# A two-layer encoder trunk on one core: the MLP's first product token-major, its convolution through DRAM copies, the gated result transposed

## The chip, the cores and the metric

The kernel runs on one core of a Trainium2 chip. The metric is the device time of one execution in microseconds (us): 2912.17 as the median of three runs, 2911.9 to 2914.39.

Names used throughout: PE is TensorE (matmuls), PEld its weight loads, DVE is VectorE, ACT is ScalarE, POOL is GpSimd, SP is SyncE. SP and POOL do no arithmetic here; they issue DMAs, each in the order of its own queue. SBUF is the on-chip memory of 128 partitions, PSUM the memory into which PE accumulates, DRAM the memory outside.

## The reference, cut to what matters

Two layers, each of three sub-layers (token mixing, cross-attention to a memory, a gated MLP), on 256 tokens of 2048 channels in float32. The change concerns the MLP:

```python
def conv_ffn(h, w_up, conv_w, conv_b, w_down):
    u = h @ w_up
    up = jnp.pad(u, ((0, 0), (1, 1), (0, 0)))
    u = up[:, :-2] * conv_w[0] + up[:, 1:-1] * conv_w[1] + up[:, 2:] * conv_w[2] + conv_b
    gate, val = u[..., :D_FF], u[..., D_FF:]
    return (jax.nn.gelu(gate, approximate=True) * val) @ w_down
```

`w_up` is 2048 x 11264 and `w_down` 5632 x 2048 (`D_FF` is 5632). So the first product has 11264 columns, 5632 for the gate and 5632 for the value. The convolution runs over tokens, three taps per channel, and the MLP is wrapped in two RMS norms:

```python
        h = rms_norm(x, ffn_pre_g[l])
        y = conv_ffn(h, w_up[l], conv_w[l], conv_b[l], w_down[l])
        x = x + rms_norm(y, ffn_post_g[l])
```

## The kernel before

**Precision.** Float32 matrices are multiplied as sums of two reduced-precision parts, hi and lo: `x` is rounded to hi, and lo is the rest. A product takes three terms: hi times hi, hi times lo, lo times hi. Weights arrive from DRAM in tiles of 128 x 1024 (512 KB, `load`, L110, issued by SP); ACT makes hi (a cast, L133) and DVE makes lo (a subtraction, L134). There are four buffers each for the loaded tile, hi and lo. Two tiles are a unit of 2048 columns. Activations stand as operands with channels on the partitions: `A_ff` is 16 row tiles of 128 channels, each hi and lo of 256 tokens.

**Two forms of product.** In the *feature-major* form (`block`, L148, called by `ws_chunk`, L163) the weights are loaded into PE and the tokens stream: L151 multiplies hi of the weights by hi and lo of the tokens in one matmul of 512 columns, L152 lo of the weights by hi of the tokens, 256 columns. The result has channels on the partitions. `merge` (L220) then adds the two halves. In the *token-major* form (`mm_rows`, L296) the tokens are loaded into PE, 128 at a time, and 512 weight columns stream: three matmuls, L301 to L303, for each of the two groups of 128 tokens. The result has tokens on the partitions. `projected` (L611) makes one column of 512 output channels in this form out of four units; `stream` (L639) runs a list of such units, makes the next unit (load, cast, split) before it uses the present one, and calls a function `between` after each row tile, into which other work is put.

**The MLP before.** The first 512 columns of `w_up`, the gate and value parts of the first two tiles of 128 channels, are token-major and belong to the sub-layer boundary (`Columns`, `boundary`), where the residual is renewed and the new operand is built; they are turned by eight transposes (L1233, `ut`). All others, 84 chunks of 128 channels per layer, are feature-major (`up`, tile `up`). With channels on the partitions, the convolution runs along the free dimension: `conv` multiplies by the norm's factor (L1190, `rb`), does the middle tap and the bias on ACT (L1192) and the outer taps on DVE as two shifted multiply-adds (L1195, L1199) with one number per channel. GELU (L1223), product (L1224) and `split` (L228, L229) give tiles of `G`, which are already in operand form for the down projection. After each quarter of `G` (11 row tiles) `products` (L371) runs that part of the down projection token-major (tile `y`), in four columns of 512 channels, and adds it up (L1252, L1254, `Out.take`).

**What sets the order.** The program is written as one sequence; a scheduler of the framework moves instructions within limits, engine by engine, before the run. On the chip each engine then works strictly in its order, and waits where an operand is not there. Only in `boundary` is the order that of the text. A layer's end prepares the first weights of the next product ahead (`ahead_apart`), and `products` holds the last matmuls of its last column back so that one group of tokens ends early.

## Time and profile before

The profiled execution took 2912.27 us, of which the profile's span covers 2910.5.

| | before |
|---|---|
| median of three runs | 2912.17 us |
| profiled execution | 2912.27 us |
| its span | 2910.5 us |
| granted TensorE clock, mean | 0.999 |
| DMA traffic, mean | 193 GB/s |
| chunks of the first product, feature-major, per layer | 84 |
| token-major columns of the first product, per layer | 1 |

A row of a group reads: line, engine, operation, tile written <- tiles read, shape out<-in, xcount | time the engine was busy with them, mean ns of one | idle time of the engine just before them and what ended it. A row of the timeline reads: start (us from the span's start), duration, engine, line, operation, count. A row on DMA issues ends with the KB of one and the median us from its issue to its landing. A stretch gives busy us of each engine. PE's matmuls are pipelined, so their durations overlap and sums of them exceed the time; the distance between starts tells the rate.

### The profile page before, as it was taken

What the parts mean: (1) busy time and instruction counts of PE and PEld (TensorE: products, weight loads), DVE (VectorE), ACT (ScalarE), POOL (GpSimd) and SP (SyncE); (2) the same over time, 40 slices, a digit from 0 to 9 for tenths busy, and PEclk for the clock granted to TensorE, in tenths of its full rate; (3) what the DMA queues carried; (4) which work ended last, traced back from release to release, by engine and by line L of the source; (5) the groups of instructions that cost most, each with busy time, mean ns of one, the idle gap of its engine ahead of it and who ended that gap; (6) DMA issues with size and microseconds to landing.
All of it is one profiled execution on the core that took longest, in us unless ns stands there. A gap on an engine that the chain in (4) does not pass through costs nothing.

```text
span 2910.5 us, 39133 instructions
## 1 busy us (share of the span) xinstructions
PE 2897.6 (100%) x14476; PEld 2443.7 (84%) x14476; DVE 2053.4 (71%) x2930; ACT 1583.6 (54%) x2479; POOL 34.9 (1%) x60
## 2 busy tenths in 40 slices
PE   9999999999999999999999999999999999999998
PEld 7888888888888888888878888888888888888887
DVE  6668767666875867767776587776678768677676
ACT  6556455555655545545555564445566555455454
POOL 0000000000000000000000000000000000000000
PEclk9999999999999999999999999999999999999999
DMA  8644776765666566565655456677556666666655
GB/s 290 188 148 159 232 235 224 226 187 160 196 184 195 187 188 191 180 200 184 212 174 182 145 163 222 222 236 215 181 159 202 187 193 186 188 190 186 195 185 163
DMA packets 161775, 563.09 MB, mean 193 GB/s; under 512 B 18480, under 2 KB 19504, under 8 KB 161584
## 3 DMA queue, kind: packets, MB, share of 16 engines
q1 hardware_dynamic: 156816, 545.53, 59.5%
q0 software_dynamic: 4480, 14.68, 1.8%
q8 instruction: 113, 1.85, 0.3%
q14 instruction: 78, 0.64, 0.1%
q10 hardware_dynamic: 288, 0.39, 0.0%
HBM read 556.34 MB, written 4.19 MB: 193 GB/s over the span
## 4 chain that ended last, share of the span: by engine, by line
PE 97%; DVE 1%; ACT 1%; DMA 0%; issue 0%; DVEq 0%; ACTq 0%
PE up L151 22%; PE up L152 11%; PE y L302 8%; PE y L303 8%; PE y L301 8%; PE g L301 4%; PE g L303 4%; PE g L302 4%; PE qk L302 3%; PE qk L303 3%; PE qk L301 2%; PE a L301 2%; PE a L303 2%; PE a L302 2%; PE as L302 2%; PE as L301 2%
## 5 line engine op out<-in xcount | busy, mean ns | idle before, releaser
L134 DVE TENSOR_TENSOR wlo<-w,whi 128x1024 fp32r<-128x1024 f32 (+1 forms) x981 | 1179.9, 1205 | 656.4 <-ACT whi L133 649.4
L133 ACT CAST whi<-w 128x1024 fp32r<-128x1024 f32 (+1 forms) x981 | 1015.6, 1037 | 955.6 <-PE y L303 295.4
L151 PE MATMUL up<-A_ff,whi 128*128 128x512 f32 x2688 | 946.3, 397 | 0.0
L152 PE MATMUL up<-A_ff,wlo 128*128 128x256 f32 x2688 | 755.0, 281 | 0.0
L151 PEld LDWEIGHTS up<-A_ff,whi 128*128 128x128 f32 x2688 | 504.9, 188 | 121.9
L152 PEld LDWEIGHTS up<-A_ff,wlo 128*128 128x128 f32 x2688 | 509.0, 189 | 0.4
L301 PE MATMUL y<-whi,G 128*128 128x512 f32 x704 | 274.3, 390 | 0.0
L302 PE MATMUL y<-wlo,G 128*128 128x512 f32 x704 | 274.2, 389 | 0.0
L303 PE MATMUL y<-whi,G 128*128 128x512 f32 x704 | 274.2, 389 | 0.0
L301 PE MATMUL g<-whi,A_mix 128*128 128x512 f32 x512 | 202.3, 395 | 0.0
L302 PE MATMUL g<-wlo,A_mix 128*128 128x512 f32 x512 | 200.8, 392 | 0.0
L303 PE MATMUL g<-whi,A_mix 128*128 128x512 f32 x512 | 200.3, 391 | 0.0
L303 PEld LDWEIGHTS y<-whi,G 128*128 128x128 f32 x704 | 132.2, 188 | 27.5
L301 PEld LDWEIGHTS y<-whi,G 128*128 128x128 f32 x704 | 132.2, 188 | 27.4
L302 PEld LDWEIGHTS y<-wlo,G 128*128 128x128 f32 x704 | 132.2, 188 | 27.2
L303 PE MATMUL qk<-whi,A_mix 128*128 128x512 f32 x320 | 125.6, 392 | 0.0
L302 PE MATMUL qk<-wlo,A_mix 128*128 128x512 f32 x320 | 125.4, 392 | 0.0
L301 PE MATMUL qk<-whi,A_mix 128*128 128x512 f32 x320 | 124.9, 390 | 0.0
L223 ACT COPY t<-up 128x256 f32<-128x256 f32 x168 | 61.7, 367 | 102.8 <-DVE G L229 84.7
L303 PEld LDWEIGHTS g<-whi,A_mix 128*128 128x128 f32 x512 | 96.3, 188 | 19.1
L301 PEld LDWEIGHTS g<-whi,A_mix 128*128 128x128 f32 x512 | 96.3, 188 | 18.4
L302 PEld LDWEIGHTS g<-wlo,A_mix 128*128 128x128 f32 x512 | 96.4, 188 | 17.9
(264 smaller groups left out, 4076.7 us busy)
## 6 DMA issues: line engine op xcount, KB each, us to landing
w<-in_w_up SPq DMA_DIRECT2D x336, 512.0 KB, 4.5
w<-in_w_dn SPq DMA_DIRECT2D x160, 512.0 KB, 4.0
w<-in_w_g SPq DMA_DIRECT2D x128, 512.0 KB, 4.3
w<-in_w_qk SPq DMA_DIRECT2D x80, 512.0 KB, 4.5
w<-in_w_ao SPq DMA_DIRECT2D x64, 512.0 KB, 5.0
w<-in_w_mo SPq DMA_DIRECT2D x64, 512.0 KB, 4.3
w<-in_w_vu SPq DMA_DIRECT2D x47, 512.0 KB, 4.5
w<-in_w_fo SPq DMA_DIRECT2D x32, 512.0 KB, 4.1
```

Source lines behind the costliest of these rows:

```text
L133: nc.scalar.copy(hi[:, :m], w[:, :m])
L134: nc.vector.tensor_sub(lo[:, :m], w[:, :m], hi[:, :m].bitcast(F32))
L151: nc.tensor.matmul(ps, hi, a, start=first, stop=False, skip_group_check=True)
L152: nc.tensor.matmul(ps[:, :T], lo, a[:, 0:T], start=False, stop=last, skip_group_check=True)
L223: nc.scalar.copy(b, ps[:, T : 2 * T])
L301: nc.tensor.matmul(ps, ah, hi, start=first, stop=False)
L302: nc.tensor.matmul(ps, ah, lo, start=False, stop=False)
L303: nc.tensor.matmul(ps, al, hi, start=False, stop=last)
```

## The change

All but the first 512 columns of `w_up` become token-major as well, as 21 further halves per layer of 512 columns (11 blocks of 512 channels, each a gate half and a value half; the gate half of block 0 is the boundary's). Each half is a `projected` item list of four units. After a half, ACT evicts both groups of tokens with the norm's factor (now a number per partition) into one of four places, `gate`, `val`, `left`, `right`. As tokens are now on the partitions, the convolution's neighbours lie on other partitions: POOL stores the half (256 x 512, 512 KB) into a DRAM tile `bounce` with a row of zeros at either end, and reads it back twice, shifted by one row, into `left` and `right`. The taps and the bias, now rows of 512 numbers, are loaded by SP to all partitions (`taps`, 1 MB per half). DVE multiplies the three copies by their taps and adds them; GELU is on ACT, the product with the gate on DVE. `turn` transposes the value half on PE, four transposes for each group of tokens, into a PSUM tile `gt`, from which ACT and DVE make hi and lo of `G`. A list `due` spreads these steps over the row tiles of the next half: each is called so many row tiles after the half's end (the middle tap at 5, left 9, right 10, sums 11 and 12, GELU or product 13, turns 14 and 15). The down projection runs after the gate halves of blocks 4 and 8 (16 row tiles each, of blocks 0 to 3 and 4 to 7, as further items of the same stream) and at the end (12 row tiles, by `products`, which takes the first eight row tiles of columns 0 and 1 first and calls `beside` after each row tile). `par` loses the taps; the host lays weights out anew.

The core of the diff:

```diff
-    def products(src, S, nk, begin, finish, last, ahead=(), made=None, mid=None):
+    def products(src, S, nk, begin, finish, last, ahead=(), made=None, mid=None, first=None, beside=None):
         late = []
-        for n in range(4):
-            begin(n)
-            pss = [psum(f"y{j}") for j in range(2)]
+        order = [(n, k0) for n in range(4) for k0 in range(0, nk, 4)]
+        if first is not None:
+            order.sort(key=lambda u: (u[0] > 1, u[0] < 2 and u[1] >= first, u))
...
+                if beside is not None:
+                    beside()
...
+    bounce = [dram.tile([T + 2, 512], F32, tag=f"bounce{i}", name="bounce", bufs=1) for i in range(2)]
+    zeros = cp.tile([2, 512], F32, tag="zeros", name="zeros")
+    nc.vector.memset(zeros, 0.0)
+    for rows in bounce:
+        nc.gpsimd.dma_start(rows[0:1], zeros[0:1])
+        nc.gpsimd.dma_start(rows[T + 1 : T + 2], zeros[1:2])
...
+        def beside(i=None):
+            now = [f for n, f in due if n == 1]
+            due[:] = [(n - 1, f) for n, f in due if n > 1]
+            for f in now:
+                f()
+
+        def taps(i):
+            if not places:
+                c, d = [big.tile([P, 8, 512], F32, tag=tag, name=name) for tag, name in (("C", "cv"), ("D", "uv"))]
+                places.update(taps=(c[:, 0:4], c[:, 4:8]), gate=d[:, 0:2], val=d[:, 2:4], left=d[:, 4:6], right=d[:, 6:8])
+            b, w = divmod(i, 2)
+            h = b + w * NB
+            to = places["taps"][w]
+            nc.sync.dma_start(to, t["conv"][l, :, h * 512 : (h + 1) * 512].partition_broadcast(P))
+            return to
+
+        def half(i):
+            b, w = divmod(i, 2)
+            def finish(j, ps, to):
+                u = places["val" if w else "gate"]
+                nc.scalar.activation(u[:, j], ps, AF.Copy, scale=pre.t[:, j : j + 1])
+                if not j:
+                    return
+                left, right = places["left"], places["right"]
+                rows = bounce[w]
+                nc.gpsimd.dma_start(rows[1 : T + 1].rearrange("(j p) n -> p j n", j=2), u)
+                nc.gpsimd.dma_start(left, rows[0:T].rearrange("(j p) n -> p j n", j=2))
+                nc.gpsimd.dma_start(right, rows[2 : T + 2].rearrange("(j p) n -> p j n", j=2))
+                def times(v, k):
+                    nc.vector.tensor_mul(v, v, to[:, k : k + 1].to_broadcast([P, 2, 512]))
+                def own():
+                    times(u, 1)
+                    nc.vector.tensor_add(u, u, to[:, 3:4].to_broadcast([P, 2, 512]))
+                def activate():
+                    if w:
+                        nc.vector.tensor_mul(u, u, places["gate"])
+                    else:
+                        nc.scalar.activation(u, u, AF.Gelu_apprx_tanh)
+                due.extend([(5, own), (9, lambda: times(left, 0)), (10, lambda: times(right, 2))])
+                due.extend([(n, lambda v=v: nc.vector.tensor_add(u, u, v)) for n, v in ((11, left), (12, right))])
+                due.append((13, activate))
+                if w:
+                    due.extend([(14, lambda: turn(0)), (15, lambda: turn(1))])
+
+            def turn(j):
+                q, k = divmod(b, DN)
+                if G[q] is None:
+                    G[q] = big.tile([P, 4 * min(DN, NB - q * DN), 2, T], F32R, tag="B", name="G")
+                pt = ps_sc.tile([P, 4, P], F32, tag="sc", name="gt")
+                for m in range(4):
+                    nc.tensor.transpose(pt[:, m], places["val"][:, j, m * P : (m + 1) * P], ident)
+                hi, lo = [G[q][:, 4 * k : 4 * k + 4, part, j * P : (j + 1) * P] for part in range(2)]
+                nc.scalar.copy(hi, pt)
+                nc.vector.tensor_sub(lo, pt, hi.bitcast(F32))
+            return finish
+
+        def up(i):
+            b, w = divmod(i, 2)
+            return projected(t["w_up"][l, b + w * NB], A, "up", half(i), lambda: taps(i))
...
+        for i in range(1, 2 * NB):
+            items += up(i)
+            b = i // 2
+            if i % 2 == 0 and b % DN == 0:
+                q = b // DN - 1
+                for n in range(4):
+                    src = down(q, n)
+                    items += projected([src[:, u * UW : (u + 1) * UW] for u in range(4)], Down(q), "y", sum_down(q, n))
...
+        steps = products(
+            [down(2, n) for n in range(4)], Down(2), 4 * (NB - 2 * DN), y.gain, lambda j, n, ps: y.take(j, n, ps, True), 4,
+            before_last, items[-1].w, mid=5, first=8, beside=beside,
+        )
```

Three places in the new order follow. In the names, `up0` and `up1` are the PSUM tiles of the two groups of tokens, `whi`, `wlo` and `w32` a weight tile's hi, lo and loaded form, `con` holds the identity, `cv` the taps, and `uv` all four places; a word such as DVE_49 or DMASW7_49 in brackets is the semaphore of an engine or DMA queue waited for.

TensorE, in layer 0's first product. Before, the end of one chunk of 128 channels (`up_8590`) and the start of the next (`up_8645`):

```order
L151 MATMUL up_8590<-A_ff_5930,whi_8586 128x512
L152 MATMUL up_8590<-A_ff_5930,wlo_8587 128x256
L151 MATMUL up_8590<-A_ff_5930,whi_8586 128x512
L152 MATMUL up_8590<-A_ff_5930,wlo_8587 128x256
L151 MATMUL up_8645<-A_ff_5930,whi_8637 128x512 [waits Activation_49]
L152 MATMUL up_8645<-A_ff_5930,wlo_8638 128x256 [waits DVE_49]
```

Now, near the end of the gate half of block 2 (`up0_6886`, `up1_6887`): the end of its seventh weight tile, 6954, and the first half of its eighth, 6958:

```order
L302 MATMUL up1_6887<-whi_6954,A_ff_5938 128x512
L303 MATMUL up1_6887<-wlo_6955,A_ff_5938 128x512
L304 MATMUL up1_6887<-whi_6954,A_ff_5938 128x512
L1275 MATMUL gt_7016<-con_95,uv_6322 128x128 [waits DVE_49,PE_49]
L1275 MATMUL gt_7016<-con_95,uv_6322 128x128 x3
L302 MATMUL up0_6886<-whi_6958,A_ff_5938 128x512 [waits Activation_49]
L303 MATMUL up0_6886<-wlo_6959,A_ff_5938 128x512
L304 MATMUL up0_6886<-whi_6958,A_ff_5938 128x512
L302 MATMUL up1_6887<-whi_6958,A_ff_5938 128x512
```

The feature-major matmuls are gone; the first turn of block 1's value half stands after seven of the eight weight tiles and waits for DVE, with the eighth tile's matmuls behind it.

VectorE, the same half: from the split of its fifth weight tile (6917) to the product with the gate. The tiles 6921, 6955 and 6959 are its sixth to eighth, 6996 is the first of the next half.

```order
L135 TENSOR_TENSOR wlo_6917<-w32_6912,whi_6916 128x1024 [waits DMAHW3_49,Activation_49]
L1251 TENSOR_TENSOR uv_6322<-uv_6322,cv_6321 128x1024 [waits DMAHW1_49,DMASW7_49]
L1255 TENSOR_TENSOR uv_6322<-uv_6322,cv_6321 128x1024 [waits DVE_49]
L135 TENSOR_TENSOR wlo_6921<-w32_6914,whi_6920 128x1024 [waits DMAHW4_49,Activation_49]
L1251 TENSOR_TENSOR uv_6322<-uv_6322,cv_6321 128x1024 [waits DMASW0_49]
L135 TENSOR_TENSOR wlo_6955<-w32_6950,whi_6954 128x1024 [waits DMAHW5_49,Activation_49]
L1251 TENSOR_TENSOR uv_6322<-uv_6322,cv_6321 128x1024 [waits DMASW1_49]
L1264 TENSOR_TENSOR uv_6322<-uv_6322 128x1024 [waits DVE_49]
L135 TENSOR_TENSOR wlo_6959<-w32_6952,whi_6958 128x1024 [waits DMAHW6_49,Activation_49]
L1264 TENSOR_TENSOR uv_6322<-uv_6322 128x1024 [waits DVE_49]
L135 TENSOR_TENSOR wlo_6996<-w32_6991,whi_6995 128x1024 [waits DMAHW7_49,Activation_49]
L1259 TENSOR_TENSOR uv_6322<-uv_6322 128x1024 [waits DVE_49]
```

The three rows of L1251 are the middle tap (it waits for the store, as it overwrites what is stored), the left and the right copy (they wait for their reads). Between the left copy and the product stand three splits of weights, and the product is what the turn above waits for.

GpSimd, two halves in a row (`bounce_325` takes value halves, `bounce_324` gate halves); before, its queue held nothing in this stretch.

```order
L1246 DMA bounce_325<-uv_6322 128x2x512 [waits DMASW2_49,DMASW3_49,DVE_49,Activation_49]
L1247 DMA uv_6322<-bounce_325 128x2x512 [waits DMASW7_49,DVE_49]
L1248 DMA uv_6322<-bounce_325 128x2x512 [waits DVE_49]
L1246 DMA bounce_324<-uv_6322 128x2x512 [waits DMASW6_49,DMASW5_49,Activation_49]
L1247 DMA uv_6322<-bounce_324 128x2x512 [waits DMASW2_49,DVE_49]
L1248 DMA uv_6322<-bounce_324 128x2x512 [waits DVE_49]
```

The store waits for the eviction on ACT, the first read for the store's landing (DMASW7 in the second row), and the second read follows the first in the queue.

More of the change, by code (lines that the diff above doesn't have):

```diff
@@ L1276, in encoder @@
+        steps = products(
+            [down(2, n) for n in range(4)], Down(2), 4 * (NB - 2 * DN), y.gain, lambda j, n, ps: y.take(j, n, ps, True), 4,
+            before_last, items[-1].w, mid=5, first=8, beside=beside,
+        )
+        for n in range(4):
+            next(steps)
         if l + 1 < L:
@@ L1397, in _layout @@
         st["w_xo"].append(_rows(i["w_xo"][l]))
[L1398 to L1402 removed]
+        st["w_up"].append(_outer(i["w_up"][l]))
+        st["w_dn"].append(_rows(i["w_down"][l]))
     a["par"] = par
```

201 lines of the change are left out of this document (81 added, 120 removed).

## The prediction

> **What bounds the kernel now.** I read the page first (busy shares and the chain that ended last), then stretches, then single instructions in the timeline.
>
> ```profile
> PE 2897.6 (100%) x14476; PEld 2443.7 (84%) x14476; DVE 2053.4 (71%) x2930; ACT 1583.6 (54%) x2479; POOL 34.9 (1%) x60
> PE 97%; DVE 1%; ACT 1%; DMA 0%; issue 0%; DVEq 0%; ACTq 0%
> 750.00:860.00 110.00, 110.00 (x624) 96.55 (x623) 91.41 (x149) 67.46 (x108) 0.00 (x0) 1.00 0.60 186
> ```
>
> The chain is TensorE almost alone. The third row is a stretch inside the MLP (us, then busy time of PE, PEld, DVE, ACT, POOL, then clock, DMA share, GB/s): PE never waits, VectorE works 91 of 110 us, the DMA engines 60%. So the first question is how fast matmuls follow each other, the second whether the new work can make PE wait.
>
> Durations of matmuls overlap, so I count starts. The first two rows are 27 pairs of the feature-major product apart, the last two 18 token-major matmuls:
>
> ```profile
> 999.87 0.40 PE L151 MATMUL up<-A_ff,whi 128*128 128x512 f32 x1
> ...
> 1009.41 0.40 PE L151 MATMUL up<-A_ff,whi 128*128 128x512 f32 x1
> ...
> 299.73 0.39 PE L302 MATMUL a<-wlo,O 128*128 128x512 f32 x1
> ...
> 303.81 0.39 PE L302 MATMUL a<-wlo,O 128*128 128x512 f32 x1
> ```
>
> A pair (768 columns) takes 9.54/27 = 353 ns; a token-major matmul (512 columns) takes 4.08/18 = 226.7 ns, or 340 ns for 768 columns. The same arithmetic is 4% cheaper token-major.
>
> **The change on TensorE.** The chain of waits, by line, gives the exact share of the old product:
>
> ```profile
> by line: PE up L151 21.5%; PE up L152 11.0%; PE y L302 7.6%; PE y L303 7.6%; PE y L301 7.6%; PE g L301 4.0%; PE g L303 4.0%; PE g L302 4.0%; PE qk L302 2.5%; PE qk L303 2.5%; PE qk L301 2.5%; PE a L301 2.0%; PE a L303 2.0%; PE a L302 2.0%;
> ```
>
> Removed: 32.5% of 2910.5 = 945.9 us for 2688 pairs. Added: 21 halves x 16 rows x 6 matmuls x 2 layers = 4032 matmuls x 226.7 ns = 914.1 us. That is **-31.8 us**. The down projection keeps its number of matmuls (44 rows x 4 x 6 per layer) and its form.
>
> Removed too: eight transposes of `ut` and four small products per layer. Added: 22 turns of four transposes per layer; the nearest is the turn of `rt`:
>
> ```profile
> 147.96 0.40 PE L302 MATMUL u<-wlo,A_mix 128*128 128x512 f32 x1
> 148.19 0.60 PE L772 MATMUL rt<-con,rot 128*128 128x128 f32 x4
> 148.55 0.48 PE L303 MATMUL u<-whi,A_mix 128*128 128x512 f32 x1
> 148.87 0.39 PE L301 MATMUL u<-whi,A_mix 128*128 128x512 f32 x1
> ...
> 743.89 1.03 PE L1233 MATMUL ut<-con,ut 128*128 128x128 f32 x8
> 744.76 0.61 PE L252 MATMUL ps_pre<-dg,ones 128*128 128x128 f32 x4
> 745.13 0.48 PE L151 MATMUL up<-A_ff,whi 128*128 128x512 f32 x1
> 745.44 0.28 PE L152 MATMUL up<-A_ff,wlo 128*128 128x256 f32 x1
> ```
>
> A turn costs 0.36 us, and the matmul behind it takes 0.32 instead of 0.23: 0.45 us. 44 turns: **+19.8 us**. The removed group costs 1.24 + 0.08 = 1.3 us per layer: **-2.6 us**. TensorE's own work falls by **14.6 us**.
>
> **The change on the other engines.** A half is now 96 matmuls, 21.76 us, in eight parts of 12 matmuls (2.72 us), one per 512 KB weight tile. Beside it:
>
> ```profile
> L134 DVE TENSOR_TENSOR wlo<-w,whi 128x1024 fp32r<-128x1024 f32 x947 | 1156.8, 1224 | 635.8 <-ACT whi L133 628.9
> L133 ACT CAST whi<-w 128x1024 fp32r<-128x1024 f32 x947 | 994.7, 1052 | 911.7 <-PE up L151 279.4 <-PE y L303 251.5 <-PE g L303 95.3
> L789 ACT ACTIVATE kug<-u,rstd_t 128x512 f32<-128x512 f32 x8 | 5.3, 682 | 2.0 <-PE u L303 2.0
> ```
>
> VectorE has 8 splits and 6 convolution steps of the same 128x1024 form, so 1.22 us each, 17.1 us; every second half a product and two differences for G more (1.22 and about 0.7 each), 19.7 us. ScalarE has 8 casts of 1.05, two evictions of 0.68, about 11 us. Both fit into 21.76 us **if VectorE never sits idle**. These steps replace the old merge, `rb`, taps and split steps, which were hidden under PE as well; their going gains nothing.
>
> What VectorE may idle for is new: store, then read back, through DRAM. POOL issues the store when the eviction is done, and the reads only when the store has landed. The trace has such transfers only in half the size:
>
> ```profile
> w<-in_w_dn SPq DMA_DIRECT2D x160, 512.0 KB, 4.0
> ...
> w<-in_w_dn SPq DMA_DIRECT2D x32, 256.0 KB, 2.7
> gb<-in_gpost POOLq DMA_DIRECT2D x24, 256.0 KB, 5.0
> gb<-in_bg POOLq DMA_DIRECT2D x16, 256.0 KB, 4.4
> ...
> rows<-mir POOLq DMA_DIRECT2D x8, 256.0 KB, 4.8
> ...
> out<-X SPq DMA_DIRECT2D x6, 256.0 KB, 2.1
> ```
>
> The second 256 KB cost 4.0 - 2.7 = 1.3 us on SP's queue. I take the store as 4.8 + 1.3 = 6.1 us and the read as 4.4 + 1.3 = 5.7 us, nearest to POOL's own store and load, 11.8 us together. The ends are POOL's shortest and longest:
>
> ```profile
> L950 POOL DMA_DIRECT2D rows<-mir x8: 544/544/547, 275.0 to 1941.0; - x8
> ...
> DMA to landing us min/median/max: 4.1/4.8/6.1
> ...
> L951 POOL DMA_INDIRECT work<-rows,mirror x8: 986/1034/1254, 281.8 to 1946.1; - x8
> ...
> DMA to landing us min/median/max: 5.0/5.3/6.0
> ...
> L336 POOL DMA_DIRECT2D gb<-in_gpost x24: 536/536/563, 477.3 to 2876.2; - x24
> ...
> DMA to landing us min/median/max: 3.3/5.0/8.0
> ```
>
> Low: 4.1 + 3.3 = 7.4 us, as if size cost nothing; high: 6.1 + 6.0 + 2 x 1.3 = 14.7 us.
>
> Now the wait, for a value half; time 0 is PE's first matmul of the next half. The last matmul starts at -0.23 and lasts 0.39; its eviction (0.68) ends at 0.85, the store goes out at about 0.95, and the left copy has landed at 0.95 + 6.1 + 0.1 + 5.7 = **12.85**. VectorE stands before the left copy with everything behind it in order: times left, split, times right, add, split, add, split, product with the gate, eight steps of 1.22, so the product ends at 22.65 (the right copy, issued some 1 us behind the left, is there before its step). PE reaches the first turn after seven parts, at 7 x 2.72 = **19.04**, and waits in order, with the eighth part behind it: 22.65 + 0.1 - 19.04 = **3.7 us**. Were the copy there at once, the four weight buffers would set the pace: the seventh part's cast waits for the end of the third part (8.16), its split follows at 9.3, and six more steps end at 9.3 + 7 x 1.22 = 17.8. So the cover is 1.2 us only. A first block of a layer has both turns one row later, at 20.4: 2.35 us. Sum: 20 x 3.7 + 2 x 2.35 = **+78.7 us**. Nothing takes it back: PE has no idle time to give.
>
> For a gate half no turn follows. There the last thing due is the split of the eighth part: left, split, right, add, split, 6.1 us, must end at 19.04, so the left copy may land until 12.94. At 12.85 this costs **nothing**, by a hair; above it each us costs 20 us. The tap rows go out on SP between two weight tiles, after the step that frees them; the weight tile behind them needs that VectorE point anyway, so they cost nothing but traffic. The four stores of zero rows at the start find an idle POOL queue. The next layer's first weights are made ready one column of the down product later; a column of 12 rows (12 x 6 x 0.2267 = 16.3 us) still lies ahead of the boundary and covers their four casts and splits.
>
> Against the profiled execution (span 2910.5, its time 2912.3, as good as the median 2912.2): 2912.3 - 31.8 - 2.6 + 19.8 + 78.7 = **2976 us**.
>
> **A page against this.** The Trainium skill, "DMA: Bandwidth & Descriptors", section "Anatomy of one DMA — SWDGE (gpsimd) path", fits one such DMA as 2.0 us plus bytes / 436e3: 3.2 us for 512 KB, 6.4 for both, and by an estimate from that page no wait at all and 2898 us. This trace does not agree: for 256 KB the page has 2.6 us, and the shortest of eight stores took 4.1.
>
> **Rivals.**
>
> *The copies come in time.* The wait vanishes where store and read together take under about 8.1 us (0.95 + 0.1 + both + 9.76 + 0.1 = 19.04). Were POOL's transfers as quick as SP's, 2.1 + 1.3 = 3.4 for the store (the row of `out`) and 4.0 for the read, 7.4 us, it would be gone: 2912.3 - 14.6 = **2898 us**, faster. Against it: all three kinds of POOL transfer have medians of 4.4 to 5.3 us at half the size. The rule on the page above gives the same end.
>
> *The DMA engines become tight.* A half moves 4 MB of weights, 0.5 stored, 1 read back and 1 of tap rows, 6.8 million bytes in some 23.7 us, 288 GB/s, where the stage now has 186:
>
> ```profile
> 0.00:40.00 40.00, 37.59 (x164) 31.00 (x165) 24.21 (x38) 28.34 (x49) 0.89 (x5) 1.00 0.92 328
> ```
>
> 328 GB/s was reached, at a share of 0.92, so it fits, but transfers then wait for each other. At the high end, 14.7 us, the left copy lands at 15.75: 6.6 us in value halves (20 x 6.6 + 2 x 5.2 = 142) and 2.8 in 20 gate halves (56): 2897.7 + 198 = **3096 us**. The Trainium skill, same page, "Specifications", has about 358 GB/s of HBM per core, which 288 stays under; no run here shows that limit.
>
> *A small wait*, store and read 8.2 to 9: up to 0.9 us x 22, **2900 to 2918**.
>
> *The change does not do what it says*: if 512 columns cost here what they cost in the old pair, 353 x 512/768 = 235 ns, 4032 x 8.6 ns = 35 us come back and the forecast becomes **3011**. Against it: the 226.7 ns of the token-major stretch above.
>
> **How the numbers follow.** Forecast with its spread of store plus read, 9 to 13.5 us (2918 to about 3050): 0.64. Copies in time: 0.13. Small wait: 0.07, nearly all within 0.2%. Tight DMA (3050 to 3100 and more): 0.13. No gain per column: 0.03. The range 2896 to 3065 leaves out some 0.12 above and a little below. 0.2% is 6 us, about what a measurement of this kernel can tell from no change: faster 0.13, same 0.07, slower 0.80.
>
> **What would show it.** Right: PE idle only in front of the turns `gt`, about 3.7 us, 22 times, released by VectorE's product; VectorE idle in front of the times-left step, released by the DMA from `bounce`; 226 to 227 ns between starts of `up`; landing of about 6 us for store and read. Wrong: `gt` without idle time (the transfers took under 4 us), or PE idle in front of `up` with casts waiting for `w_up` (DMA tight), or wide spacing of `up`. The forecast falls first with the landing times: 1 us in their sum is 22 us.

## The result and the profile after

| | before | after |
|---|---|---|
| median | 2912.43 us (4 runs) | 3052.71 us (4 runs, 3046.24 to 3057.78) |
| span of the profiled execution | 2910.5 us | 3044.5 us |
| granted TensorE clock, mean | 0.999 | 0.984 |
| DMA traffic, mean | 193 GB/s | 223 GB/s |

The change makes the kernel slower: after to before is 1.048, with a 95% interval of 1.0455 to 1.0504. The forecast was 2976 us. So the direction was right, but the loss, 134 us between the spans, is twice the 64 us of the forecast. One of all the runs below, one of eleven of the last experiment, took 3557 us at a mean clock of 0.761 and is left out of that experiment's ratio. The page of the profile after, engines and chain:

```profile
PE 2935.6 (96%) x13284; PEld 2416.5 (79%) x13284; DVE 2027.9 (67%) x2353; ACT 1477.5 (49%) x2083; POOL 131.1 (4%) x196
PE 67%; DMA 15%; DVE 8%; issue 6%; ACT 4%; POOL 0%; SPq 0%; DVEq 0%; ACTq 0%; POOLq 0%
```

PE was 97% of the chain; now a third of it is something else, DMA above all, and PE is no longer busy all the time. The view of waits after (engine, line, waited for: us in all, times, longest) says where PE and VectorE stand:

```profile
PE gt L1275 <- DVE uv L1259: 76.3, 21, 5.2
PE up L303 <- DVE wlo L135: 17.0, 26, 2.1
...
DVE uv L1251 <- DMA uv<-bounce: 110.9, 44, 4.7
DVE uv L1251 <- DMA bounce<-uv: 70.6, 25, 5.3
```

The first row is the wait that the forecast named: PE before the turn `gt`, 3.6 us each time. The second is one that it did not: PE before a weight's lo part, in the middle of a product. The last two are what is behind both: VectorE stands 181 us before the copies and before the store (70.6 us, which the forecast did not price), which must have landed before the own factor's step may overwrite the half. One value half shows it, on VectorE (start, duration, operation, idle time before and its releaser). PE's first matmul of the next half starts at 864.26:

```profile
869.56 1.23 DVE L135 TENSOR_TENSOR wlo<-w,whi 128x1024 fp32r<-128x1024 f32 x1
874.06 1.23 DVE L1251 TENSOR_TENSOR uv<-uv,cv 128x1024 f32<-128x1024 f32 x1 [3.27 <-DMA bounce<-uv]
875.32 1.23 DVE L1255 TENSOR_TENSOR uv<-uv,cv 128x1024 f32<-128x1024 f32 x1
876.46 1.22 DVE L135 TENSOR_TENSOR wlo<-w,whi 128x1024 fp32r<-128x1024 f32 x1
879.04 1.23 DVE L1251 TENSOR_TENSOR uv<-uv,cv 128x1024 f32<-128x1024 f32 x1 [1.36 <-DMA uv<-bounce]
...
886.99 1.22 DVE L1259 TENSOR_TENSOR uv<-uv 128x1024 f32<-128x1024 f32 x1
```

VectorE is free at 870.8, stands for the store until 874.06 and for the left copy until 879.04. That is 14.8 us after PE's first matmul of the next half, where the forecast had 12.85. Most of the difference arises before the transfers begin, on ScalarE (ACT):

```profile
863.09 1.98 ACT L134 CAST whi<-w 128x1024 fp32r<-128x1024 f32 x2
864.97 1.25 ACT L1241 ACTIVATE uv<-up,rstd_t 128x512 f32<-128x512 f32 x2
866.52 0.72 POOL L1246 DMA_DIRECT2D bounce<-uv  x1 [16.63 <-ACT uv L1241]
```

The eviction stands behind two casts in ACT's order, so the store goes out at 2.3 us instead of 0.95. After the left copy the eight steps run without a break, and the product ends at 888.21. On PE, at the same time:

```profile
883.85 0.39 PE L304 MATMUL up<-whi,A_ff 128*128 128x512 f32 x1
888.35 1.09 PE L1275 MATMUL gt<-con,uv 128*128 128x128 f32 x4 [4.11 <-DVE uv L1259]
...
890.09 0.63 PE L304 MATMUL up<-whi,A_ff 128*128 128x512 f32 x1
890.52 0.63 PE L302 MATMUL up<-whi,A_ff 128*128 128x512 f32 x1
```

PE waits 4.11 us, and the matmuls behind the wait follow each other at 0.43 us instead of 0.227. The view of stretches (us, busy time of PE, PEld, DVE, ACT and POOL, then clock, DMA share, GB/s) names the reason; the first row is the stretch ahead of the wait, the second the end of the wait and what follows it:

```profile
876.00:883.00 7.00, 6.52 (x29) 5.06 (x29) 5.64 (x6) 2.50 (x3) 0.00 (x0) 1.00 0.73 235
886.20:893.00 6.80, 4.65 (x15) 3.98 (x16) 4.88 (x5) 0.73 (x3) 0.00 (x0) 0.50 0.94 283
```

The granted clock is 0.50 there. Up to PE's last matmul it stands at 0.5 for 95.6 us in all, in twenty pieces. In the kernel before, its record, which begins at 5.8 us, falls to 0.5 only after the last matmul.

To split the loss, the distances between starts of PE's instructions are set, one by one, against those of the run without copies that follows below (span 2896.0, no such waits): 79.8 us in front of `gt`, 37.7 us of matmuls and transposes at half rate (the waits themselves left out), 26.3 us of gaps between matmuls of `up` outside those pieces (late weight splits), and 4.7 us elsewhere, most of it at the layers' ends. That is 148.5 us, the whole difference between 2896.0 and 3044.5. PE waits for a late split 28 times, 20.5 us in all by the view of waits. 23 of these waits, 18.4 us, come after a value half and 5, 2.1 us, after a gate half.

### The profile page after: what moved, and what is told of

Same layout as the page of the kernel before. It is cut to its first block, busy times and chain, and to the rows that moved or that the text cites. A ratio compares the mean times of both kernels' runs of the same rounds, so it can differ in the third digit from the quotient of the medians.

```text
span 3044.5 us, 35918 instructions
## 1 busy us (share of the span) xinstructions
PE 2935.6 (96%) x13284; PEld 2416.5 (79%) x13284; DVE 2027.9 (67%) x2353; ACT 1477.5 (49%) x2083; POOL 131.1 (4%) x196
## 4 chain that ended last, share of the span: by engine, by line
PE 67%; DMA 15%; DVE 8%; issue 6%; ACT 4%; POOL 0%; SPq 0%; DVEq 0%; ACTq 0%; POOLq 0%
DMA uv<-bounce 7%; PE y L303 7%; PE y L304 7%; PE y L302 7%; DMA bounce<-uv 7%; PE g L302 4%; PE g L303 4%; PE g L304 4%; DVE uv L1264 3%; PE qk L303 2%; PE qk L304 2%; PE qk L302 2%; PE up L302 2%; PE up L303 2%; PE up L304 2%
## 5 line engine op out<-in xcount | busy, mean ns | idle before, releaser
L303 PE MATMUL up<-wlo,A_ff 128*128 128x512 f32 x1344 | 537.3, 400 | 17.2 <-DVE wlo L135 17.0
L302 PE MATMUL up<-whi,A_ff 128*128 128x512 f32 x1344 | 539.8, 402 | 0.0
L304 PE MATMUL up<-whi,A_ff 128*128 128x512 f32 x1344 | 532.6, 396 | 0.0
L303 PEld LDWEIGHTS up<-wlo,A_ff 128*128 128x128 f32 x1344 | 259.5, 193 | 81.9 <-DVE wlo L135 30.1
L304 PEld LDWEIGHTS up<-whi,A_ff 128*128 128x128 f32 x1344 | 258.8, 193 | 54.3
L302 PEld LDWEIGHTS up<-whi,A_ff 128*128 128x128 f32 x1344 | 259.6, 193 | 53.2
L1251 DVE TENSOR_TENSOR uv<-uv,cv 128x1024 f32<-128x1024 f32 x132 | 161.4, 1222 | 182.2 <-DMA uv<-bounce 110.9
L1275 PE MATMUL gt<-con,uv 128*128 128x128 f32 x176 | 38.3, 361 | 76.3 <-DVE uv L1259 76.3
```

Source lines behind the costliest of these rows:

```text
L302: nc.tensor.matmul(ps, ah, hi, start=first, stop=False)
L303: nc.tensor.matmul(ps, ah, lo, start=False, stop=False)
L304: nc.tensor.matmul(ps, al, hi, start=False, stop=last)
L1251: nc.vector.tensor_mul(v, v, to[:, k : k + 1].to_broadcast([P, 2, 512]))
L1275: nc.tensor.transpose(pt[:, m], places["val"][:, j, m * P : (m + 1) * P], ident)
```

## The experiments

Theory A: PE loses time because VectorE stands, in its strict order, before a transfer that has not landed; the product and the weight splits queued behind it are late, and each long wait of PE also halves its clock. Rival B: the traffic itself (2.5 MB per half beside 4 MB of weights) makes the weights late. The tables of steps in the diffs are numbers of row tiles after a half's end, 1.36 us each.

### What is the halved clock worth? (e1_fill)

Sixteen matmuls whose result nothing reads stand ahead of the first turn in blocks 0 to 9, so that PE works instead of waiting.

```diff
             def turn(j):
...
+                if j == 0 and b < NB - 1:
+                    fill = psum_pt("fill")
+                    for m in range(16):
+                        nc.tensor.matmul(fill, A[:, m, 0, 0:P], flat(A, m), start=True, stop=True)
```

> In front of the first turn of 20 of the 22 value halves PE is given 16 more matmuls of 512 columns whose result nobody reads (16 x 0.2267 = 3.6 us each, 73 us of work in all). Theory: the idle time in front of a turn costs twice, once as such (3.7 us) and once because the granted clock is 0.5 for one to three windows of 3.4 us afterwards; the added work fits into the idle time, the clock stays at 0.99 or more, and the time falls by what the halved clock took, 0.016 x 3045 / 2 = 24 us, to about 3028 us. Rival: the lower clock has another cause or costs nothing; then the time stays at 3045 to 3060, or rises where the added work doesn't fit.

3028.12 us, ratio to before 1.0396 (1.0378 to 1.0413); mean clock 0.996, and 17.1 us at half clock instead of 95.6. Some 73 us of useless matmuls made the kernel 24.6 us faster. So the halved clock is a real cost. That the time meets the expected 3028 us is partly luck. The 72.5 us of added work and the 15.3 us of waits that are left in front of `gt` exceed the 76.3 us of waits that they replace, so the clock was worth more than the 24.6 us, as the count from the starts says too.

### Fewer bytes or fewer trips (e4_no_taps, e3_no_store_wait, e6_sbuf, e7_sbuf_later)

First the factors are loaded only for the first two halves of a layer, 1 MB per half less:

```diff
-            nc.sync.dma_start(to, t["conv"][l, :, h * 512 : (h + 1) * 512].partition_broadcast(P))
+            if i < 2:
+                nc.sync.dma_start(to, t["conv"][l, :, h * 512 : (h + 1) * 512].partition_broadcast(P))
```

> The tap rows are loaded for the first two halves of a layer only (the later halves use these, so the convolution's factors are not the real ones): 1 MB less traffic in 20 of 22 halves, 42 MB in all. Theory (latency): the chain of store and read stays, its transfers get a little shorter (some 0.5 us each), the waits shrink by about a quarter: 3015 to 3040 us. Rival (the DMA engines are tight, and what makes transfers long is the tap traffic): store and read fall to 4.5 us and under, late weights vanish, and the time falls below 2990 us.

3047.47 us, 1.0465 (1.0448 to 1.0483), against 1.0479 with all factors: hardly a change, and less of one than theory A had expected too (3015 to 3040). This traffic costs next to nothing.

Second, the reads take input that does not depend on the store:

```diff
-                nc.gpsimd.dma_start(left, rows[0:T].rearrange("(j p) n -> p j n", j=2))
-                nc.gpsimd.dma_start(right, rows[2 : T + 2].rearrange("(j p) n -> p j n", j=2))
+                nc.gpsimd.dma_start(left, t["xt"][:, :, 0:512])
+                nc.gpsimd.dma_start(right, t["xt"][:, :, 512:1024])
```

> The left and right copies are read from an input in DRAM (same size, same 2 KB rows) in place of bounce, so the reads no longer wait for the store; the store stays, and the neighbours in the convolution are not the real ones. Traffic is unchanged. Theory (latency of two transfers in a row): the left copy lands some 5 us earlier, PE's wait in front of gt falls from 78 us to under 15, the halved clock with it, and most late weight splits, since VectorE no longer stands in front of the left copy: 2905 to 2935 us. Rival (the DMA engines are tight): weight tiles still land late and the time stays above 2960 us.

2988.09 us, 1.0268 (1.0247 to 1.0289), a miss for A's number. No wait is left in front of `gt`, but these reads land later themselves (median 8.3 us for the left one instead of 6.0), and VectorE stands longer than before (257 us against 181):

```profile
DVE uv L1251 <- DMA uv<-in_xt: 214.7, 76, 8.2
DVE uv L1251 <- DMA bounce<-uv: 42.2, 23, 5.3
```

So it tells little: it changed the landing time along with the trip.

Third, the shifted copies go from SBUF to SBUF, with no store:

```diff
-                nc.gpsimd.dma_start(rows[1 : T + 1].rearrange("(j p) n -> p j n", j=2), u)
-                nc.gpsimd.dma_start(left, rows[0:T].rearrange("(j p) n -> p j n", j=2))
-                nc.gpsimd.dma_start(right, rows[2 : T + 2].rearrange("(j p) n -> p j n", j=2))
+                nc.gpsimd.dma_start(left[1:P], u[0 : P - 1])
+                nc.gpsimd.dma_start(left[0:1, 1], u[P - 1 : P, 0])
+                nc.gpsimd.dma_start(right[0 : P - 1], u[1:P])
+                nc.gpsimd.dma_start(right[P - 1 : P, 0], u[0:1, 1])
```

> The shifted copies go from SBUF to SBUF in one trip (127 rows in one transfer, the odd row in a second), with no store to DRAM; the places of the steps are those of the changed kernel. Theory A (the two trips one after the other, 10.7 us, are what is late): copies land 6 to 8 us after the half's end, ahead of the ninth step (12.2 us), so no `gt` wait, no halved clock, few late splits: 2905 to 2930 us. Rival B (traffic): bytes fall by 1 MB in 3 per half, waits shrink by a third, 2990 to 3010 us. Rival C (a transfer inside SBUF is as slow as the two trips): 3040 us.

3041.53 us, 1.0448 (1.0431 to 1.0466): rival C. The landing times in this run (us from issue), of the left copy's 127 rows:

```profile
DMA to landing us min/median/max: 4.6/7.2/10.9
```

And of the right copy's:

```profile
DMA to landing us min/median/max: 7.4/9.1/12.7
```

One trip inside SBUF takes as long as a store or a read through DRAM (medians 4.7 and 6.0 after the change) and more, and the right copy's last row comes later still. With later steps as well it gave 3018.4 us (1.0363, 1.0346 to 1.0380), where A had expected 2900 to 2920. Bytes and trips are not the way in.

### Later calls (e2_later, e5_all_later)

First the turns alone, then all steps, for all blocks but the last:

```diff
-                    due.extend([(14, lambda: turn(0)), (15, lambda: turn(1))])
+                    n = 20 if b < NB - 1 else 14
+                    due.extend([(n, lambda: turn(0)), (n + 1, lambda: turn(1))])
```

> The two turns of a value half are called 20 and 21 row tiles after its end in place of 14 and 15, in all blocks but the last of each layer. Theory: the wait in front of the turn is the main loss; 20 waits of 3.7 us and 20 stretches of halved clock (1.1 us each) go, 96 us, so about 2957 us; what is left over TensorE's own 2898 is two waits at the last blocks (10 us) and weight splits that come late (some 30 to 45 us). Rival: VectorE is the bound in these halves and the wait only moves in front of up (on wlo); then the time stays above 3020 us.

> All convolution steps of a half come later (own factor 8 instead of 5, left copy 11 instead of 9, right 12, sums 13 and 14, Gelu or product 15, turns 20 and 21), but for the last block. Theory A (VectorE stands before the left copy, with weight splits queued behind it, and that is what is left in the run with later turns, about 57 us of gaps between `up` matmuls): the gaps fall to 10 to 20 us, no `gt` wait but in the last block, 2920 to 2945 us. Rival B (the weights themselves come late, since the copies and factors take the DMA engines): VectorE's waits move, the gaps stay, 2965 to 2985 us.

2980.30 us (1.0231, 1.0214 to 1.0248) and 2978.18 us (1.0228, 1.0211 to 1.0245). The first misses its expected 2957 us by 23. The wait in front of `gt` is gone, and the clock is back at 0.997 and 0.996. But 57 us of gaps between matmuls of `up` remain in both, more than after the change, and moving all steps won nothing over moving the turns: A's number for the second was missed by 33 us, and its result lies in B's range. At this point B was alive.

### Neither copies nor traffic, then traffic alone (e8_no_copies, e9_traffic_only)

The eight VectorE steps stay at their places with the half itself as operand. The first run has no store and no reads; the second has both, but the store takes other data and nothing reads the copies.

```diff
-                nc.gpsimd.dma_start(rows[1 : T + 1].rearrange("(j p) n -> p j n", j=2), u)
+                nc.gpsimd.dma_start(rows[1 : T + 1].rearrange("(j p) n -> p j n", j=2), places["taps"][w][:, 0:2])
...
-                due.extend([(5, own), (9, lambda: times(left, 0)), (10, lambda: times(right, 2))])
-                due.extend([(n, lambda v=v: nc.vector.tensor_add(u, u, v)) for n, v in ((11, left), (12, right))])
+                due.extend([(5, own), (9, lambda: times(u, 0)), (10, lambda: times(u, 2))])
+                due.extend([(n, lambda: nc.vector.tensor_add(u, u, u)) for n in (11, 12)])
```

> No store to DRAM and no shifted copies; the eight VectorE steps of a half stand at their places with the half itself as operand (the neighbours of the convolution are left out). Both theories: no step waits for a transfer, 1.5 MB per half less traffic, so no `gt` wait, full clock, and few late splits: 2896 (before's 2910.5 less 14.6) to 2920 us. If it stays above 2950 us, neither waits nor traffic of the copies carry the loss, but the work or its order does.

> As the run without copies, but with all their traffic: the store writes the same bytes out of the factors' tile, and both shifted reads go where they went, unread (the neighbours are left out as there). Theory A (VectorE stands in its order before a copy, with splits behind it): no more than 10 us over the run without copies, 2900 to 2925 us. Rival B (the traffic itself makes weights late): 50 us and more over it, 2950 to 2990 us.

2897.25 us (0.9950, 0.9934 to 0.9967) and 2898.41 us (0.9957, 0.9940 to 0.9973). The same stretch of the MLP, without any copies:

```profile
750.00:860.00 110.00, 110.00 (x494) 91.11 (x493) 89.43 (x80) 54.76 (x58) 0.00 (x0) 1.00 0.71 238
```

And with their traffic:

```profile
750.00:860.00 110.00, 110.00 (x494) 91.10 (x493) 90.38 (x81) 53.12 (x58) 10.68 (x15) 1.00 0.89 315
```

PE works through in both; 315 GB/s at a DMA share of 0.89 cost it nothing. In this run the store waits for the factors and not for an eviction, so the traffic lies elsewhere in a half (a store at 866.34, evictions at 872.46 and 894.23). But the last run below has its stores and reads behind the evictions, with 308 GB/s in this stretch, and PE is busy for 109.64 of the 110 us there too. So B falls. And the span of 2896.0 us in the first is the span before less 14.5 us: the forecast's sum of PE work (14.6 us less) is shown.

### One wait at a time (e12_store_wait, e13_copy_wait)

With traffic only, but the store of the half itself, so that only the own factor's step waits (first edit below, to the changed kernel); then the store of other data, but steps that read the copies (second edit).

```diff
-                due.extend([(5, own), (9, lambda: times(left, 0)), (10, lambda: times(right, 2))])
-                due.extend([(n, lambda v=v: nc.vector.tensor_add(u, u, v)) for n, v in ((11, left), (12, right))])
+                due.extend([(5, own), (9, lambda: times(u, 0)), (10, lambda: times(u, 2))])
+                due.extend([(n, lambda: nc.vector.tensor_add(u, u, u)) for n in (11, 12)])
```

```diff
-                nc.gpsimd.dma_start(rows[1 : T + 1].rearrange("(j p) n -> p j n", j=2), u)
+                nc.gpsimd.dma_start(rows[1 : T + 1].rearrange("(j p) n -> p j n", j=2), places["taps"][w][:, 0:2])
```

> As the run with traffic only, but the store is of the half itself, so that the own factor's step waits for it; copies land unread (the neighbours are left out). Theory A (the left copy, two trips away, is what stands in the way): 2898 to 2915 us, the store's wait being 25 of 44 halves at 2.8 us with a part of 5.4 us in hand. Rival (the store's wait alone makes the late splits): 2930 us and more.

> As the run with traffic only, but the steps read the left and right copies and wait for them; the store is of the factors' tile, so the own factor's step waits for nothing (the neighbours are factors, not the half's). Theory A: nearly the whole loss is here, `gt` waits of 3 to 4 us with the halved clock behind them, 3010 to 3045 us. Rival (both waits are needed to make a late product): 2930 to 2990 us.

2923.78 us (1.0033, 1.0020 to 1.0046) and 2933.97 us (1.0075, 1.0060 to 1.0090). The first misses A's range upwards: the store's wait alone costs some 25 us over the run with traffic only, by 46.3 us of VectorE standing in 33 halves:

```profile
DVE uv L1251 <- DMA bounce<-uv: 46.3, 33, 5.4
...
PE gt L1275 <- DVE uv L1259: 16.1, 11, 4.6
```

The second misses A's range (3010 to 3045) and lies in the rival's, but does not settle its question: its store no longer depends on the half, so the copies do not start at the half's end, and the scheduler moved steps ahead into the boundary, where PE waits 16.4 us for a renewed residual. VectorE stands 186.8 us before its copies there, no less than after the change, and the run takes only 36 us more than the one with traffic only. So the sum of VectorE's standing does not measure the loss; it depends on the place in the order where VectorE stands.

### The whole computation, with the waits covered (e10, e11, e14, e15, e16, e17, e18)

If A holds, the whole kernel must come near 2897 us once VectorE meets each transfer after it has landed. The gate's half gets a pair of tiles that turn over, so that its steps may come later (own factor 10, copies 12 and 13, sums 14 and 15, product 17, turns 20 and 21):

```diff
-                u = places["val" if w else "gate"]
+                if not j:
+                    state["u"] = [places["val"]] if w else [tmp2("gate").rearrange("p a n -> p (a n)") for _ in range(2)]
+                us = state["u"]
...
+                at = (10, 12, 13, 14, 15, 17, 20) if i < 2 * NB - 1 else (5, 9, 10, 11, 12, 13, 14)
```

> The whole computation, with the gate's half in a pair of tiles that turn over, so that every step may come later: own factor at 10 (13.6 us after the half's end), left copy 12, right 13, sums 14 and 15, Gelu or product 17, turns 20 and 21, but for the last block. Theory A: VectorE stands before almost nothing, 2905 to 2935 us. Rival B (traffic): within 10 us of the runs with later turns, 2965 to 2985 us.

3031.08 us (1.0406, 1.0389 to 1.0424). It is spoilt: the factors of the next half but one are loaded before the right copy's step, which then takes those, and VectorE waits 85.9 us for them. With the factors loaded by a step of their own (e11), and with the last block covered too (e14: three of four columns take their first 8 row tiles ahead of its turn):

```diff
+                if i + 2 < 2 * NB:
+                    due.append((18, lambda: ready.append(taps(i + 2))))
...
-            order.sort(key=lambda u: (u[0] > 1, u[0] < 2 and u[1] >= first, u))
+            order.sort(key=lambda u: (u[0] > 2, u[1] >= first and u[0] < 3, u))
```

> The whole computation. As the run with two gates, but a half's factors are loaded by a step of their own at 18 after the half before the last has ended, when its tile has been read (in the run with two gates they were loaded ahead of the right copy's step, which then waited for them and took the wrong ones). Steps: own factor 11, left copy 13, right 14, sums 15 and 16, Gelu or product 17, turns 20 and 21, but for the last block. Theory A (what costs time is only VectorE and PE standing before what has not landed): VectorE stands before next to nothing, the last block's wait and halved clock stay (about 10 us in both layers), 2902 to 2925 us. Rival (late steps find the transfers later too): above 2950 us.

> The whole computation. As the run with the factors loaded by a step of their own, and in the last block as well: three of the four column groups of the last down product take their first 8 rows ahead of the last block's turn (24 parts of 1.36 us instead of 16), with the third in the two PSUM banks that nothing else uses there, so that its steps may be as late as the others'; what is prepared for the next layer comes one column group later. Theory A: no `gt` wait at all, 2896 to 2912 us, within 0.2 per cent of the run without copies if nothing new is late. Rival (the next layer's first weights, prepared one group later, are late): 5 to 10 us more at the layer's end.

3008.08 us (1.0316, 1.0297 to 1.0334) and 3002.51 us (1.0309, 1.0295 to 1.0323), both far outside A's ranges. I then blamed SP, where the factors' load waited 145 us ahead of weight loads, and moved it from 18 to 26:

> The whole computation. As the run that covers the last block, but a half's factors are loaded at 26 instead of 18 (their tile has been read at 14): on SP's queue their issue stood 145 us in 40 waits for VectorE, up to 9.5 us, with weight loads behind it. Theory A (that queue is what held the two last whole kernels at 3002 and 3008 us): the waits on SP and the late weights go, 2900 to 2925 us. Rival (VectorE's waits for copies and store, 190 us there, are what counts, wherever the factors are issued): 2970 to 3000 us.

3006.07 us (1.0313, 1.0295 to 1.0332), again far from A's 2900 to 2925, and SP's wait was still 135 us. A run with the own factor's step two places later and all that follows four (e16) gave 3107.0 us, but there the copies' tiles had already been given to the next half, and its steps took that half's copies. With the reads called later this was mended:

```diff
-                nc.gpsimd.dma_start(left, rows[0:T].rearrange("(j p) n -> p j n", j=2))
-                nc.gpsimd.dma_start(right, rows[2 : T + 2].rearrange("(j p) n -> p j n", j=2))
+                def copies():
+                    nc.gpsimd.dma_start(left, rows[0:T].rearrange("(j p) n -> p j n", j=2))
+                    nc.gpsimd.dma_start(right, rows[2 : T + 2].rearrange("(j p) n -> p j n", j=2))
...
+                at = (13, 17, 18, 19, 20, 21, 24) if i < 2 * NB - 1 else (12, 15, 16, 17, 18, 19, 22)
+                due.extend([(6, copies), (at[0], own), (at[1], lambda: times(left, 0)), (at[2], lambda: times(right, 2))])
```

> The whole computation. In the run before, the left and right tiles were already given to the next half's reads (issued at 16) when the steps at 17 and 18 took them, so that these took and waited for the next half's copies; here the reads are issued at 6, so the tiles are free until 22. All else as there. Theory A: VectorE's waits for copies and store fall under 60 us, 2900 to 2930 us. Rival (the transfers keep coming later than VectorE, which runs ahead of PE): 2960 to 3010 us, as in the runs with two gates.

3032.96 us (1.0405, 1.0391 to 1.0420), outside A's range and the rival's (2960 to 3010). Its VectorE rows, for a gate half evicted from 885.47 on, explain the series:

```profile
896.20 1.22 DVE L135 TENSOR_TENSOR wlo<-w,whi 128x1024 fp32r<-128x1024 f32 x1
902.56 1.23 DVE L1265 TENSOR_TENSOR uv<-uv,cv 128x1024 f32<-128x1024 f32 x1 [5.14 <-DMA uv<-bounce]
904.94 1.22 DVE L1265 TENSOR_TENSOR uv<-uv,cv 128x1024 f32<-128x1024 f32 x1 [1.16 <-DMA uv<-bounce]
906.08 1.22 DVE L135 TENSOR_TENSOR wlo<-w,whi 128x1024 fp32r<-128x1024 f32 x1
...
907.36 0.50 PE L303 MATMUL up<-wlo,A_ff 128*128 128x512 f32 x1 [3.75 <-DVE wlo L135]
```

The left copy's step is called at 17, which is 23 us after the half's end, yet VectorE comes to it 12 us after the eviction began (897.4), stands 5.14 us, and PE then waits 3.75 us for the split behind it. The calls were moved, but the order on VectorE was not: that is the scheduler's. In all the kernels with later calls and real copies except e16, the first two (2980 and 2978 us) included, VectorE was free for the left step at a median of 10.4 to 13.7 us after the eviction began, with three weight splits before the own factor's step and one or two more before the left one, wherever they were called; after the change it was 9.3 us in gate halves and 12.8 in value halves. The copy landed at medians of 12.8 to 16.2 us.

So the last run forces the order by data: one column of the half and of each copy takes a sum with zero times a column of a weight's hi part, which ACT can make only when PE has come far enough.

```diff
+        def held(v, part):
+            i = at_item[0]
+            if i is not None and i + 1 < len(items):
+                hi = items[i + 1].w.parts[part][0]
+                nc.vector.scalar_tensor_tensor(
+                    out=v, in0=hi[:, 0:1].bitcast(F32), scalar=0.0, in1=v, op0=ALU.mult, op1=ALU.add
+                )
```

> The whole computation. In all runs with later steps VectorE came to the left copy's step 11.9 to 13.7 us after the half's end and to the own factor's at 4.6 to 7.1 us, wherever the code called them: the order on VectorE is the scheduler's. Here it is forced: one column of the half and of both copies first takes a sum with zero times a column of a weight's upper part, which ACT makes only when PE has freed its tile (the unit of calls 12 to 15 for own, 16 to 19, second piece, for left and right), so left and right come behind three more weight splits, at about 17 us; two gates, last block covered, own factor 9, copies 13 and 14, sums 15 and 16, product 17, turns 20 and 21, factors loaded at 20. Theory A (VectorE must come to a step after its transfer has landed): its waits for copies and store fall from 180 to under 60 us, 2900 to 2930 us. Rival (transfers then land later again): 2960 us and more.

**2907.68 us, 0.9983 of before (0.9974 to 0.9992).** The whole computation is 145 us faster so than in the change as made, and 0.17% faster than in the kernel before. The nearest run without the forced order is e14 (3002.51 us). It calls the own factor's step at 11 instead of 9 and the factors' load at 18 instead of 20, and has no added sums; all else is the same, so the order on VectorE is worth some 95 us. Its page:

```profile
PE 2886.4 (99%) x13284; PEld 2391.3 (82%) x13284; DVE 2045.7 (70%) x2611; ACT 1483.6 (51%) x2105; POOL 140.5 (5%) x218
PE 93%; DMA 3%; DVE 2%; ACT 1%; issue 1%; POOL 0%; SPq 0%; DVEq 0%; ACTq 0%; POOLq 0%
```

A value half on VectorE, with the added column sums (L1223) and the first of the two copies' steps behind them:

```profile
866.97 1.23 DVE L135 TENSOR_TENSOR wlo<-w,whi 128x1024 fp32r<-128x1024 f32 x1 [0.32 <-ACT whi L134]
868.12 0.22 DVE L1223 SCALAR_TENSOR_TENSOR uv<-whi,uv 128x1 f32<-128x1 f32 x2
868.30 1.23 DVE L1273 TENSOR_TENSOR uv<-uv,cv 128x1024 f32<-128x1024 f32 x1
```

No idle time stands before the copies' steps. VectorE now comes to the left one at a median of 19.4 (value halves) and 20.4 us (gate halves), when the copy has been there for 3 to 4, and five splits stand before the own factor's step, three more before the left one. The transfers are no faster than before (reads 6.7 us in the median, stores 7.2 to 7.6), and the traffic is the same. VectorE's waits for store and copies fall from 181 us to 19, and PE's are small:

```profile
DVE uv L1273 <- DMA uv<-bounce: 6.9, 2, 3.5
DVE gate L1223 <- DMA bounce<-gate: 6.4, 4, 3.2
...
PE gt L1314 <- DVE uv L1296: 3.1, 4, 1.5
PE up L303 <- DVE wlo L135: 1.7, 1, 1.7
```

Theory A is shown by this pair of facts: all traffic with no waits costs nothing (2898), and the whole computation with the waits moved behind the landing is within 10 us of that. That run also covers the last block and has the second gate tile; what each of these two is worth in it was not measured apart.

## Why the prediction was right or wrong, point by point

| step of the prediction | forecast, us | measured, us |
|---|---|---|
| TensorE's own work | -14.6 | -14.5 (span without copies) |
| wait at the turns `gt` | +78.7 | +79.8 |
| gate halves (the term of the sum), and splits behind value halves (not in it) | 0 | +26.3 |
| clock | not in the sum | +37.7 |
| elsewhere, mostly layers' ends | 0 | +4.7 |
| sum | +64 | +134 |

Two steps failed: the sum put nothing on weight splits that come late behind a value half, and nothing on the clock after PE has idled. With 26.3 and 37.7 us, these make 64 of the 70 us that are missing.

*TensorE's work.* Right. The 226.7 ns of a token-major matmul hold: 3783 of 3988 distances between matmuls of `up` lie between 220 and 240 ns. The rival that the change brings no gain per column is out.

*The wait at the turns.* Right in mechanism and place: 21 waits, released by VectorE's product. The size is right partly by luck. (Times are from PE's first matmul of the next half, medians of the 22 value halves unless said.) In value halves the store and the left read together took 12.0 us in the median from the store's issue, against 11.9 in the forecast, though each was off: the store 7.4 us instead of 6.1 (3.4 after gate halves), the left read 4.5 instead of 5.7 (7.1 after gate halves). But the store went out at 2.7 us instead of 0.95, since the eviction stood behind casts on ACT in 15 of the 22 value halves. The prediction had shown that ACT's busy time fits into a half and had not asked for its order. So the left copy landed at 15.2 us instead of 12.85. Against this, VectorE's eight steps took 9.2 us instead of 9.8, as they start 1.13 us apart, and PE came to the turn at 20.6 us instead of 19.04. What is left is a wait of 4.1 us in the median instead of 3.7. The prediction did not count that the own factor's step waits for the store; this alone took 70.6 us of VectorE's time.

*"At 12.85 this costs nothing, by a hair; above it each us costs 20 us."* For gate halves this nearly held: the copy landed at 13.15 us in the median, 0.2 over the limit, and PE waited 2.1 us in all for late splits after them. What failed is that the splits were looked at for gate halves alone. After a value half VectorE stands first for the store and then for the left copy, with weight splits behind each; 18.4 of PE's 20.5 us of waits for a late split are there. The runs with later calls show the price when nothing else hides it, 57 us.

*"Nothing takes it back: PE has no idle time to give."* Here the sum stopped too soon. The idle time of PE is not only lost itself: of the 20 waits at `gt` of over a microsecond, the 18 of about 3 us or more were each followed by matmuls at half the rate, the two of 2.1 and 2.6 us were not. Three more pieces at half clock began behind late splits of 1.9 to 2.2 us. That is 37.7 us, and the run with useless matmuls shows that it is the idling that costs it.

*Factors, zero rows, the next layer's weights: nothing.* Right for the factors as far as tried (about 5 us without them). Elsewhere 4.7 us were lost, 3.9 of them in front of the last down products, whose split stood behind VectorE's steps for the last value half.

*Rivals.* "Copies in time" (2898) did not happen, but its price was right to a microsecond: the runs without waits gave 2897 and 2898. The page of the Trainium skill that spoke for it, "DMA: Bandwidth & Descriptors", section "Anatomy of one DMA — SWDGE (gpsimd) path", with 3.2 us for 512 KB, does not agree with the medians of 4.7 to 6.6 here. "DMA tight" had 3050 to 3100 us and more, into which the result falls, but not for its reason: store and left read took 12.0 us together and not 14.7, and the traffic alone costs nothing.

## What to carry to other kernels

An engine that works in strict order and stands before a DMA holds up everything behind it, so a transfer's landing belongs in that engine's order and not in the number of steps by which the code calls it later: read from the trace when the engine really comes to the step, and force the order by a data dependency where the scheduler would not keep it. When a change puts waits of some 2 us or more before TensorE, add the time at half clock behind them. Ask not only how long a transfer takes but when it goes out, from the order of the engine that releases it. And before blaming traffic, run the traffic with nothing waiting for it.

## What the runs showed of the hardware

The granted clock of TensorE fell to 0.50 for pieces of 3.41, 6.82 or 10.24 us (886.20 to 893.02 in the half shown), in a kernel that keeps PE 96% busy. All twenty pieces begin on one grid of 3.41 us, and what decides is how long PE was idle within one window of that grid: at least 1.86 us in the window ahead of every piece, and at most 1.80 us in every other window at full clock. So single waits of 1.9 to 2.2 us were enough three times, while the waits of 2.1 and 2.6 us at `gt`, each of which fell into two windows, were not. In the traces of all runs, their first 10 us left out, a window with over 1.92 us of idle time was always followed by half clock and one with under 1.64 us never. The Trainium skill, "TensorE: Matmul & The Clock Gate", section "HAM oscillation — how this bites in real kernels", gives the rule that gaps of over some 3.4 us must be avoided; the trace agrees with the length of the window, but not with 3.4 us as the gap that may be left.

A copy of 127 rows (508 KB) between partitions inside SBUF, shifted by one, landed after 7.2 us in the median, no sooner than a store to DRAM (4.7 us) or a read from it (6.0 us) of about the same size. And a DMA share of 0.89 with 315 GB/s left the weights in time for PE throughout.
